# Triangular inversion from blocks of 16, finer bursts, and low parts on GpSimd in a recurrent stage

## The chip, the cores and the metric

One of a Trainium2 chip's cores runs the whole program. The metric is the device time of one execution in microseconds (us), the median of several runs. The engines are called PE (TensorE), DVE (VectorE), ACT (ScalarE), POOL (GpSimd) and SP (SyncE) in the profile.

## The reference, cut to what matters

Two transformer-like blocks work on 512 tokens of width 1024 in float32. The first block (two layers of attention and a gated feed-forward part) isn't touched by the change. The second holds an RWKV-7 time mix, a 31-tap causal convolution with a layer norm, a merge of both, and another feed-forward part:

```python
def wkv7(r, w, k, v, a, b):
    def step(S, inp):
        r_t, w_t, k_t, v_t, a_t, b_t = inp
        sa = jnp.einsum('bhvk,bhk->bhv', S, a_t)
        S = S * w_t[:, :, None, :] + sa[..., None] * b_t[:, :, None, :] + v_t[..., None] * k_t[:, :, None, :]
        y = jnp.einsum('bhvk,bhk->bhv', S, r_t)
        return S, y
    _, ys = lax.scan(step, S0, seq)
...
y_rwkv, v_first = rwkv7_time_mix(h, p_r, p_k, p_v, ...)
y_conv = conformer_conv(p_c, ...)
merged = jax.nn.sigmoid(z_rwkv) * y_rwkv + jax.nn.sigmoid(z_conv) * y_conv
x = x + rms_norm_2(merged @ w_out[i], post_mix_norm[i])
```

There are 16 heads of 64 columns. The kernel cuts the 512 steps of the scan into 8 chunks of 64 tokens. Within a chunk the steps become products with the inverse of a unit triangular 64x64 matrix, one for each head and chunk; between chunks the state S is carried on.

## The kernel before

**Products.** Float32 products are made of three passes in the float32r format: a weight tile `raw` is split into a high part `wh` (ScalarE copies it with rounding) and a low part `wl` (the rest, a subtraction). `wsplit` does this for weights, and the table `W["sub"]` says which engines take turns at the subtraction: VectorE alone outside of the recurrent stage, VectorE and GpSimd alternately in it. `dense` makes one unit of the stage: 24 products of 128x128 by 128x512 into one PSUM bank, 16 with the high part and 8 with the low part.

**The recurrent stage.** The function `tile_two_blocks` ends its second half with `drive`, which writes out the stage's order by hand. TensorE and VectorE keep the order in which the program issues their instructions. The table `units` lists 72 dense units in order: the convolution's inputs (c), the pairs of heads (i), the gates (g), the output maps of the time mix (w) and of the convolution (m). Between their products `drive` lets seven streams advance, as bursts of small instructions: `outs` (twice), which prepare one pair of heads each (`pair_out`); `solves`, which inverts the triangular matrices of a group of two pairs (`solve`, four groups); `chains`, which carries the state over 8 chunks (`chain`); `posts`, which normalizes a group's result; `mapped_rows`; and `ends`, which holds the convolution's layer norm. The w units need all four posts, apart from the first part of w0 and w1, which fill up the last chain; the m units need the layer norm.

**The planner's clock.** `Clock` holds a planned time for each engine, with a cost for each operation. A stream goes on when its last burst is done by that clock. `dense` yields after every second product, with True for a minor stop, at which streams that wait for a full burst (BURST or FREE) don't go on; full stops come where the count `n` of products is a multiple of 8. VectorE's spare time is given to the convolution's taps (`conv`, 8 x 30 multiply-adds on 128x512, tile `acc`): `taps.until(t)` issues taps as long as VectorE's planned end stays before `t`, which is TensorE's planned time minus 1 us. What GpSimd and ScalarE do follows from the order in which the streams issue it.

**The solve.** The diagonal 8x8 blocks of the matrices are gathered from a DRAM copy (`abd`) by four DMAs, inverted by forward substitution on VectorE (7 steps of a product and a sum, tile `x`), written back (`ttd`) and fetched as 32x32 blocks (`dd`, transposed `dt`). Then TensorE doubles the block size: `quad` makes 64 products of 32x32 (16 matrices on four 32-row strips), with the identity added in by a product of `ident` where `eye` is set. From 8 to 16 this takes the products dt,e and dd,de and de,dd; from 16 to 32 dt,RA and again dd,de and de,dd; from 32 to 64 the products RA and rr,dT. The tile `e` holds the entries of a 16x16 block that lie outside of its 8x8 blocks, scaled by a mask on ScalarE.

**The chain.** For each chunk: products of SV and X; ScalarE and VectorE copy half of the result each into SV; GpSimd scales the state (`ds`); products of SV and BKT; VectorE adds them to `ds` as the next SV; products with RA give the output.

**The layer norm's mean.** GpSimd adds each finished `acc` to `asum`. When all taps are done, a product with `oneD` makes the mean, VectorE subtracts it from 8 tiles, ScalarE squares them (`sq`), VectorE sums (`ssum`), and a product makes the variance.

The profile puts most instructions of the stage on a helper's lines: L192 is the recorder of TensorE's products, L152 that of the other engines, so groups are told apart by their tiles.

## Time and profile before

| | us |
|---|---|
| runs: median (lowest to highest) | 2426.93 (2425.42 to 2431.42) |
| profiled execution, own time | 2429.3 |
| its span | 2427.5 |
| TensorE, VectorE, ScalarE, GpSimd busy | 2313.3, 1198.5, 965.3, 339.0 |
| mean granted clock of TensorE | 0.969 of full speed |
| recurrent stage | about 1268 to 2005 |

The page begins with the busy time of each engine and its share of the span. "PEld" is TensorE's loading of weights, which runs beside its products. A row of the timeline has the start, the duration, the engine, the line, the operation with its tiles (output<-inputs), the shapes and the number of instructions merged in it; a bracket gives the engine's idle time ahead of it and what ended that. A row of the waits says who waited for whom. A product of float32 tiles that isn't split has two records in the profile.

### The profile page before, as it was taken

The page shows a single profiled execution, that of the slowest core. Times are in us where ns is not written, and L with a number is a line of the kernel's source. Part 1 is how long each engine was busy: PE and PEld are TensorE (multiplying, and loading weights), DVE is VectorE, ACT ScalarE, POOL GpSimd, SP SyncE. Part 2 cuts the span into 40 slices and gives each one's busy share as a digit, 9 for nine tenths or more (in the row PEclk, how much of TensorE's full clock was granted, in tenths as well). Part 3 has the DMA queues.
Part 4 walks back from the last instruction along what each step waited for, and adds up shares of the span by engine and source line. Part 5 has one row for each costly group of instructions (what it writes and reads, how often), then busy time and mean ns, then how long its engine had stood idle before and what let it go on. Part 6 is the DMA issues. An engine that isn't in the chain of part 4 may idle for free. (4 is left out here: it accounts for less than half of the span.)

```text
span 2427.5 us, 38347 instructions
## 1 busy us (share of the span) xinstructions
PE 2313.3 (95%) x15723; PEld 1862.5 (77%) x15723; DVE 1198.5 (49%) x1832; ACT 965.3 (40%) x1743; POOL 339.0 (14%) x457
## 2 busy tenths in 40 slices
PE   7899999999999999999999889999998699999998
PEld 6756788888798788888887677777776577888886
DVE  4366533234523653223355767778786655422232
ACT  4355423123434543222334645456633523322221
POOL 1000120000200000000012332354333221000000
PEclk9889999999999999999999899999999799999999
DMA  7330673224453144333232232234244254433331
GB/s 205 100 88 18 173 223 109 78 86 131 130 148 105 61 129 123 99 96 96 87 98 88 82 82 76 62 110 112 76 114 156 83 156 165 139 96 96 97 100 55
DMA packets 326543, 262.60 MB, mean 108 GB/s; under 512 B 47152, under 2 KB 294004, under 8 KB 325984
## 3 DMA queue, kind: packets, MB, share of 16 engines
q1 hardware_dynamic: 308552, 211.18, 29.9%
q10 hardware_dynamic: 9080, 22.37, 3.2%
q0 software_dynamic: 8736, 26.61, 3.1%
q8 instruction: 123, 2.02, 0.3%
q14 instruction: 52, 0.43, 0.1%
HBM read 225.81 MB, written 34.31 MB: 107 GB/s over the span
## 5 line engine op out<-in xcount | busy, mean ns | idle before, releaser
L186 PE MATMUL p<-hT_h,wh 128*128 128x512 f32 (+1 forms) x1376 | 511.8, 377 | 7.9 <-ACT qT L186 5.8
L186 DVE TENSOR_TENSOR wl<-raw,wh 128x1024 fp32r<-128x1024 f32 (+1 forms) x270 | 319.6, 1187 | 400.0 <-ACT wh L186 352.6
L186 PE MATMUL p<-hT_l,wh 128*128 128x512 f32 (+1 forms) x1376 | 511.4, 376 | 0.0
L186 ACT ACTIVATE wh<-raw 128x1024 fp32r<-128x1024 f32 (+1 forms) x270 | 275.8, 1025 | 547.6 <-PE p L186 370.6
L186 PE MATMUL p<-hT_h,wl 128*128 128x512 f32 (+1 forms) x1376 | 327.2, 375 | 0.0
L186 PEld LDWEIGHTS p<-hT_h,wh 128*128 128x128 f32 x1376 | 260.8, 190 | 56.3 <-ACT qT L186 6.2
L186 PEld LDWEIGHTS p<-hT_l,wh 128*128 128x128 f32 x1376 | 261.0, 190 | 46.9 <-issue 0.6
L186 PEld LDWEIGHTS p<-hT_h,wl 128*128 128x128 f32 x1376 | 247.5, 189 | 46.5 <-DVE wl L186 0.2
L186 POOL TENSOR_SCALAR rstd<-ss 128x1 f32<-128x1 f32 x52 | 18.6, 358 | 1467.0 <-ACT junk L186 1466.8
L152 DVE SCALAR_TENSOR_TENSOR acc<-c,dwc,acc 128x512 f32<-128x512 f32 x240 | 209.8, 877 | 6.7
L186 PE MATMUL p<-wh,fh 128*128 128x512 f32 x528 | 205.7, 390 | 0.7 <-DVE prm L186 0.7
L186 PE MATMUL p<-wl,fh 128*128 128x512 f32 x528 | 205.8, 390 | 0.0
L186 PE MATMUL p<-wh,fl 128*128 128x512 f32 x528 | 205.2, 389 | 0.0
L192 PE MATMUL p<-hT_h,wh 128*128 128x512 f32 x448 | 188.8, 421 | 2.9 <-ACT ls L152 2.1
L192 PE MATMUL p<-hT_l,wh 128*128 128x512 f32 x448 | 180.7, 403 | 0.6 <-issue 0.6
L186 DVE TENSOR_TENSOR fT<-sg,p 128x384 f32<-128x384 f32 (+1 forms) x88 | 46.8, 552 | 254.3 <-PE p L186 247.5
L192 PE MATMUL p<-hT_h,wl 128*128 128x512 f32 x448 | 120.6, 413 | 2.6 <-DVE wl L152 2.6
L152 ACT ACTIVATE wh<-raw 128x1024 fp32r<-128x1024 f32 (+1 forms) x78 | 77.4, 992 | 114.2 <-PE p L192 57.3
L186 DVE TENSOR_TENSOR fl<-fT,fh 128x512 fp32r<-128x512 f32 x66 | 45.1, 691 | 145.4 <-ACT fh L186 145.4
L186 PEld LDWEIGHTS p<-wh,fh 128*128 128x128 f32 x528 | 99.1, 188 | 21.5 <-ACT fh L186 0.9
L186 PEld LDWEIGHTS p<-wh,fl 128*128 128x128 f32 x528 | 99.1, 188 | 20.4
L186 PEld LDWEIGHTS p<-wl,fh 128*128 128x128 f32 x528 | 99.1, 188 | 20.3
(304 smaller groups left out, 3546.1 us busy)
## 6 DMA issues: line engine op xcount, KB each, us to landing
raw<-in_w_gu SPq DMA_DIRECT2D x88, 512.0 KB
raw<-in_w_in SPq DMA_DIRECT2D x56, 512.0 KB
raw<-in_w_down SPq DMA_DIRECT2D x44, 512.0 KB
raw<-in_ffn_w_gate SPq DMA_DIRECT2D x22, 512.0 KB
raw<-in_ffn_w_up SPq DMA_DIRECT2D x22, 512.0 KB
raw<-in_ffn_w_down SPq DMA_DIRECT2D x22, 512.0 KB
raw<-in_w_in_b SPq DMA_DIRECT2D x20, 512.0 KB
xs<-xt POOLq DMA_DIRECT2D x19, 512.0 KB, 4.2
```

Of the source, the lines that this page charges most:

```text
L152: return f(*a, **k)
L186: return f(*a, **k)
L192: return f(*a, **k)
```

## The change

It changes five things in the recurrent stage:

- The substitution on VectorE inverts 16x16 blocks: 15 steps of a product and a sum in place of 7, gathered and written back by two DMAs each in place of four, into tiles of 16x16 elements. The doubling from 8 to 16 goes, and with it the tile `e`, its scaled copies and the products dt,e and one dd,de and one de,dd of each solve.
- A full stop of `dense` comes after every fourth product.
- In the stage GpSimd alone makes the low parts.
- Taps are issued up to 1.5 us after TensorE's planned time.
- The planner's fixed cost of a tap (and of the other operations of that kind) goes from 0.21 to 0.26 us.

```diff
--- before.py
+++ after.py
@@ -125,7 +125,7 @@
             n, wide = math.prod(out.shape), len(out.shape) > 2 and out.shape[-1] < P
             return 0.65 if engine == "POOL" else 0.4 if not wide else 0.8 if n == 8192 else 0.65
         if engine == "DVE":
-            return (0.21 if op == "scalar_tensor_tensor" else 0.14) + n * (0.00215 if op.endswith("scan") else 0.00107)
+            return (0.26 if op == "scalar_tensor_tensor" else 0.14) + n * (0.00215 if op.endswith("scan") else 0.00107)
         if engine == "ACT":
             return 0.17 + n * 0.00086
         if op == "memset":
@@ -1008,7 +1008,7 @@
         i32 = blk[:, P + 1 : P + 33]
         centre = blk[:, P + 35 :]
         BANKS.update(ps=[0, 1, 2], po=[3, 4, 5], ca=[6], cb=[7])
-        W["sub"] = [nc.vector, nc.gpsimd]
+        W["sub"] = [nc.gpsimd]
         es2 = ExitStack()
         es2.enter_context(lows)
         el = es2.enter_context(tc.tile_pool(name="el", bufs=1))
@@ -1075,7 +1075,7 @@
                         nc.tensor.matmul(ps, lhsT=h[:, k, :], rhs=xl(k), start=False, stop=False)
                     n += 2 - part
                     if n % 2 == 0 and (n < 3 * len(ks) or len(ks) < KD):
-                        yield n % 8 != 0
+                        yield n % 4 != 0
             return ps
 
 
@@ -1319,9 +1319,9 @@
             def q32(i):
                 return slice(32 * i, 32 * i + 32)
 
-            def d8(t, r):
-
-                return bass.AP(t.tensor, t.offset + 264 * r, [[1024, 64], [32, 8], [1, 8]])
+            def d16(t, r):
+
+                return bass.AP(t.tensor, t.offset + 528 * r, [[1024, 64], [32, 16], [1, 16]])
 
             def quad(lhsT, rhs, eye=False):
 
@@ -1343,31 +1343,25 @@
             diag = [ABf[q32(i), :, q32(i % 2)] for i in range(4)]
 
             x = s2("x").rearrange("p q t -> p (q t)")
-            at, tt = (x[:, 128 * i : 128 * i + 128].rearrange("p (m a b) -> p m a b", m=2, a=8) for i in range(2))
-            pr = x[:, 256:]
-            nc.gpsimd.memset(tt, 0.0)
-            nc.gpsimd.memset(tt.rearrange("p m a b -> p m (a b)")[:, :, ::9], 1.0)
+            at, tt = (x[:, 256 * i : 256 * i + 256].rearrange("p (a b) -> p a b", a=16) for i in range(2))
+            pr = s2("pr").rearrange("p q t -> p (q t)")
+            nc.gpsimd.memset(x[:, 256:], 0.0)
+            nc.gpsimd.memset(x[:, 256::17], 1.0)
             yield from there(ab)
-            for r in range(4):
-                nc.sync.dma_start(at[64 * (r // 2) : 64 * (r // 2) + 64, r % 2], d8(ab, r))
-
-            e = s2("e")
-            nc.gpsimd.memset(e, 0.0)
+            for r in range(2):
+                nc.sync.dma_start(at[64 * r : 64 * r + 64], d16(ab, r))
+
             for i in range(4):
-                for m in range(2):
-                    cols = slice(16 * m + 8, 16 * m + 16)
-                    nc.scalar.activation(e[q32(i), :, cols], diag[i][:, :, cols], AF.Copy,
-                                         scale=blk[q32(i), P + 33 + m : P + 34 + m])
                 nc.gpsimd.memset(diag[i][:, :, 0:16], 0.0)
                 nc.scalar.activation(diag[i][:, :, 16:], diag[i][:, :, 16:], AF.Copy, scale=blk[q32(i), P : P + 1])
             yield from there(at)
-            for t in range(1, 8):
-                p4 = pr[:, : 2 * t * t].rearrange("p (m j s) -> p m j s", m=2, s=t)
-                nc.vector.tensor_tensor(p4, tt[:, :, :t, :t], at[:, :, None, :t, t].to_broadcast([P, 2, t, t]), ALU.mult)
-                nc.vector.tensor_reduce(tt[:, :, :t, t], p4, AX.X, ALU.add)
+            for t in range(1, 16):
+                p3 = pr[:, : t * t].rearrange("p (j s) -> p j s", s=t)
+                nc.vector.tensor_tensor(p3, tt[:, :t, :t], at[:, None, :t, t].to_broadcast([P, t, t]), ALU.mult)
+                nc.vector.tensor_reduce(tt[:, :t, t], p3, AX.X, ALU.add)
             yield from there(tt)
-            for r in range(4):
-                nc.sync.dma_start(d8(td, r), tt[64 * (r // 2) : 64 * (r // 2) + 64, r % 2])
+            for r in range(2):
+                nc.sync.dma_start(d16(td, r), tt[64 * r : 64 * r + 64])
             yield from there(td)
             dd, dt = s2("dd"), s2("dt")
             for i in range(4):
@@ -1376,15 +1370,6 @@
             nc.vector.transpose(dt, dd)
             yield BURST
 
-            de = s2("de")
-            nc.scalar.activation(de, quad(of(e), of(dt), True), AF.Copy)
-            yield BURST
-            dd_, dt = s2("dd"), s2("dt")
-            nc.scalar.activation(dt, quad(of(dd), of(de)), AF.Copy)
-            yield FREE
-            nc.scalar.activation(dd_, quad(of(de), of(dd)), AF.Copy)
-            dd = dd_
-            yield BURST
             de = s2("de")
             nc.scalar.activation(de, quad(lambda i: diag[i], of(dt), True), AF.Copy)
             yield BURST
@@ -1789,7 +1774,7 @@
             def stand():
                 t = clock.free("PE")
                 clock.t["PE"] = min([s[1] for s in streams if s[1] > t] + [t + 0.5])
-                taps.until(clock.t["PE"] - 1)
+                taps.until(clock.t["PE"] + 1.5)
                 burst()
 
             raws = [u[0]() for u in units[:2]]
@@ -1809,7 +1794,7 @@
                     if more and (at_ == SPLIT or (n == 3 and not units[i][4:])):
                         nxt, more = units[i + 1][1](raws.pop(0)), False
                     burst(at_ is True)
-                    taps.until(clock.free("PE") - 1)
+                    taps.until(clock.free("PE") + 1.5)
                 if more:
                     nxt = units[i + 1][1](raws.pop(0))
                 hl = nxt
```

The order of instructions moves throughout the stage. Three places follow, word for word as a listing of each engine's instructions has them; "..." stands for rows left out, and the number behind a tile tells buffers apart.

TensorE in the last solve, before; the rows with `SV`, `X` and `RA` are a chain's (`hT_h`, `wh`, `wl` are a dense unit's):

```order
L192 MATMUL p_15359<-blk,ident 128x512
L192 MATMUL p_15359<-dt,e 32x32 x64
...
L192 MATMUL p_15344<-RA_13394,SV_12896 64x64 x4
L192 MATMUL p_15453<-de,dd 32x32 x64
L192 MATMUL p_15329<-hT_h,wl 128x512 x8
L192 MATMUL p_15531<-SV_12896,X_12895 64x64 x4
L192 MATMUL p_15532<-X_12895,SV_12896 64x64 x4
L192 MATMUL p_15548<-dd,de 32x32 x64
...
L192 MATMUL p_15644<-blk,ident 128x512
L192 MATMUL p_15644<-dt,RA_14477 32x32 x64
```

The same place now:

```order
L192 MATMUL p_14867<-hT_l,wh 128x512
L192 MATMUL p_14874<-blk,ident 128x512
L192 MATMUL p_14874<-dt,RA_14046 32x32 x64
L192 MATMUL p_14941<-RA_12916,blk 128x512
...
L192 MATMUL p_14867<-hT_l,wh 128x512
L192 MATMUL p_14962<-de,dd 32x32 x64
L192 MATMUL p_14867<-hT_h,wh 128x512
...
L192 MATMUL p_15036<-dd,de 32x32 x64
```

The products dt,e and a first de,dd and dd,de are gone, the solve begins with dt,RA, and the pieces of a dense unit between its steps are four products long. Over the whole stage the 1728 large products stand in 126 pieces; they stood in 108.

VectorE at the end of the last chain, before (`acc` are taps, `SV` the chain's, `r` the last post's statistics, `asum` and `ssum` the layer norm's):

```order
L152 COPY SV_13826<-p_16621 64x2x64
L152 SCALAR_TENSOR_TENSOR acc<-c,dwc,acc 128x512
L152 TENSOR_TENSOR SV_13826<-p_16621,ds 64x2x64 x2
L152 SCALAR_TENSOR_TENSOR acc<-c,dwc,acc 128x512
L152 COPY SV_13826<-p_16649 64x2x64
L152 SCALAR_TENSOR_TENSOR acc<-c,dwc,acc 128x512 x3
L152 TENSOR_SCALAR r_16689<-p_16684 128x8
L152 TENSOR_SCALAR r_16696<-p_16691 128x8
L152 TENSOR_TENSOR RA_16389<-RA_16389,asum 128x512 x3
L152 TENSOR_TENSOR ssum<-ssum,sq 128x512
```

The same place now:

```order
L152 SCALAR_TENSOR_TENSOR acc<-c,dwc,acc 128x512 x2
L152 TENSOR_TENSOR SV_13419<-p_15777,ds 64x2x64 x2
L152 SCALAR_TENSOR_TENSOR acc<-c,dwc,acc 128x512 x2
L152 COPY SV_13419<-p_15823 64x2x64
L152 SCALAR_TENSOR_TENSOR acc<-c,dwc,acc 128x512 x7
L152 TENSOR_SCALAR r_15887<-p_15882 128x8
L152 TENSOR_SCALAR r_15894<-p_15889 128x8
L152 SCALAR_TENSOR_TENSOR acc<-c,dwc,acc 128x512 x2
L152 TENSOR_TENSOR RA_15581<-RA_15581,asum 128x512 x3
L152 TENSOR_TENSOR ssum<-ssum,sq 128x512
```

Nine taps stand behind the last copy of SV, where three stood, and two of them behind the statistics. On TensorE the last chain's first step stands after 1248 large products (before: 1272), its last one after 1360 (before: 1380).

GpSimd during the last chain, before (`ds` is the chain's scaled state, `wl` a low part, the DMA rows are stores):

```order
L152 TENSOR_TENSOR wl<-raw,wh 128x1024
L152 DMA zd_9677<-zsg 128x512
L152 TENSOR_TENSOR ds<-SV_13826,D_13828 64x128 x2
L152 DMA yd_9631<-RA_13394 128x512
L152 DMA zd_9678<-zsg 128x512
L152 TENSOR_TENSOR ds<-SV_13826,D_13828 64x128 x2
L152 DMA yd_9632<-RA_13394 128x512
L152 TENSOR_TENSOR ds<-SV_13826,D_13828 64x128 x2
L152 TENSOR_TENSOR wl<-raw,wh 128x1024
L152 DMA zd_9679<-zsg 128x512
L152 TENSOR_TENSOR ds<-SV_13826,D_13828 64x128
```

The same place now:

```order
L152 TENSOR_TENSOR ds<-SV_13419,D_13421 64x128 x2
L152 TENSOR_TENSOR wl<-raw,wh 128x1024
L152 DMA zd_9677<-zsg 128x512
L152 TENSOR_TENSOR ds<-SV_13419,D_13421 64x128 x2
L152 DMA ad_9663<-acc 128x512
L152 TENSOR_TENSOR asum<-asum,acc 128x512
L152 DMA zd_9678<-zsg 128x512
L152 TENSOR_TENSOR ds<-SV_13419,D_13421 64x128 x2
L152 TENSOR_TENSOR wl<-raw,wh 128x1024
L152 TENSOR_TENSOR ds<-SV_13419,D_13421 64x128 x2
L152 TENSOR_TENSOR wl<-raw,wh 128x1024
L152 DMA zd_9679<-zsg 128x512
```

There is a low part between most steps of the chain now. Of the stage's low parts of 128x1024, GpSimd makes 70 and all four of w_out's; it made 33 and two of w_out's.

## Rows read from the trace of the kernel before

**Rows 1.** Page, part 1, whole span: busy us (share) and instructions by engine
```profile
PE 2313.3 (95%) x15723; PEld 1862.5 (77%) x15723; DVE 1198.5 (49%) x1832; ACT 965.3 (40%) x1743; POOL 339.0 (14%) x457
```

**Rows 2.** Windows, recurrent stage: stretch; busy us by engine; clock, DMA share, GB/s
```profile
1268.00:2005.00 737.00, 674.34 (x7683) 527.84 (x7682) 516.65 (x755) 377.54 (x693) 249.81 (x275) 0.95 0.34 99
```

**Rows 3.** Waits of TensorE, 1268 to 2005: total us, times, longest
```profile
PE p L192 <- DVE ssum L152: 12.3, 1, 12.3
PE p L192 <- DVE RA L152: 10.6, 9, 3.1
PE p L192 <- DVE SV L152: 7.2, 6, 4.0
...
PE p L192 <- DVE wl L152: 5.4, 2, 2.8
```

**Rows 4.** Groups, TensorE, stage: busy us, mean ns | idle before
```profile
L192 PE MATMUL p<-de,dd 32*32 32x32 f32 x1024 | 11.4, 195 | 2.2 <-issue 2.1
L192 PE MATMUL p<-dd,de 32*32 32x32 f32 x1024 | 10.9, 193 | 1.5 <-issue 1.3
...
L192 PE MATMUL p<-blk,ident 128*128 128x512 f32 x16 | 8.7, 626 | 0.0
...
L192 PE MATMUL p<-dt,e 32*32 32x32 f32 x512 | 5.1, 193 | 0.0
```

**Rows 5.** Timeline, TensorE, undisturbed: start us, us, engine, line, operation
```profile
1409.02 1.98 PE L192 MATMUL p<-hT_h,wl 128*128 128x512 f32 x8
1410.84 0.39 PE L192 MATMUL p<-hT_h,wh 128*128 128x512 f32 x1
```

**Rows 6.** Timeline, TensorE, eight large products between bursts
```profile
1845.42 0.50 PE L192 MATMUL p<-hT_h,wh 128*128 128x512 f32 x1
...
1847.47 0.45 PE L192 MATMUL p<-SV,X 128*64 128x64 f32 x8
```

**Rows 7.** Timeline, VectorE, steps of the first solve
```profile
1393.53 0.16 DVE L152 TENSOR_TENSOR x<-x 128x2 f32<-128x2 f32 x1
1393.72 0.16 DVE L152 TENSOR_REDUCE x<-x 128x2 f32<-128x2 f32 x1
...
1400.05 0.33 DVE L152 TENSOR_TENSOR x<-x 128x98 f32<-128x98 f32 x1
1400.41 0.26 DVE L152 TENSOR_REDUCE x<-x 128x14 f32<-128x98 f32 x1
```

**Rows 8.** Groups by line, VectorE, stage
```profile
L152 DVE SCALAR_TENSOR_TENSOR acc<-c,dwc,acc 128x512 f32<-128x512 f32 x240 | 209.8, 877 | 6.7
L152 DVE TENSOR_TENSOR wl<-raw,wh 128x1024 fp32r<-128x1024 f32 x37 | 51.4, 1389 | 1.2 <-ACT wh L152 1.0
```

**Rows 9.** Groups by line, GpSimd, stage
```profile
L152 POOL TENSOR_TENSOR wl<-raw,wh 128x1024 fp32r<-128x1024 f32 x33 | 83.7, 2535 | 134.2 <-ACT wh L152 67.2 <-PE p L192 53.4 <-ACT RA L152 13.3
```

**Rows 10.** Timeline, VectorE, beside a low part on GpSimd
```profile
1555.90 4.32 DVE L152 SCALAR_TENSOR_TENSOR acc<-c,dwc,acc 128x512 f32<-128x512 f32 x3
...
1560.92 0.60 DVE L152 TENSOR_TENSOR SV<-p,ds 64x128 f32<-64x128 f32 x2
```

**Rows 11.** Timeline, GpSimd, the same stretch
```profile
1557.12 2.56 POOL L152 TENSOR_TENSOR wl<-raw,wh 128x1024 fp32r<-128x1024 f32 x1 [3.33 <-ACT RA L152]
```

**Rows 12.** Timeline, TensorE, same stretch (idle before it in brackets)
```profile
1561.67 0.45 PE L192 MATMUL p<-SV,X 128*64 128x64 f32 x8 [0.95 <-DVE SV L152]
```

**Rows 13.** Timeline, TensorE, end of the last chain and the layer norm
```profile
1879.80 0.45 PE L192 MATMUL p<-SV,BKT 128*64 128x64 f32 x8 [0.88 <-DVE SV L152]
...
1881.32 0.45 PE L192 MATMUL p<-SV,X 128*64 128x64 f32 x8 [0.69 <-DVE SV L152]
...
1901.81 1.87 PE L192 MATMUL p<-oneD,ssum 128*128 128x2 f32 x8 [12.29 <-DVE ssum L152]
```

**Rows 14.** Timeline, VectorE, the same end
```profile
1882.63 2.32 DVE L152 SCALAR_TENSOR_TENSOR acc<-c,dwc,acc 128x512 f32<-128x512 f32 x3
...
1894.20 0.69 DVE L152 TENSOR_TENSOR ssum<-ssum,sq 128x512 f32<-128x512 f32 x1 [2.63 <-ACT sq L152]
```

## The prediction

> **What bounds the kernel now.** I read the profile's first part, then the sums of the recurrent stage, then who TensorE waits for, then the rows of the instructions that the change touches. TensorE is busy for 95% of the span, every other engine for half of it or less [rows 1]. The change touches only the recurrent stage, which runs from about 1268 to 2005 us. There TensorE is busy for 674.3 of 737 us and VectorE for 516.7, at a mean granted clock of 0.95 [rows 2]. So most of the stage is bounded by the amount of work on TensorE, because large products fill what the recurrence leaves free; some 63 us are waits. The reader is to see in the waits that VectorE ends nearly all of the long ones, and that the largest, 12.3 us for ssum, lies in the layer norm at the end, where no product is left to fill with [rows 3].
>
> **The change part by part.** I count instructions in the order of before and of the change, take durations from the rows, and make the sum against the profiled execution's own time, 2429.3 us (span 2427.5 and 1.8 around it). The median of the runs, 2426.93, lies 2.4 below it.
>
> (a) *One doubling less.* Each of the four solves loses three of its six 64-matmul steps and one of two identity products. The profile counts twice as many records as instructions here. By their rows: all of dt,e (5.1 us), half of de,dd (11.4 busy and 2.2 waiting before them), half of dd,de (10.9 and 1.5), half of blk,ident (8.7) [rows 4]: 5.1 + 6.8 + 6.2 + 4.35 = 22.4 us. These lie between large products on the busy engine, with nothing beside them on TensorE, so I count all: **-22.4**. ScalarE loses the evacuations and the scaled copies, too; it is no bound here, so nothing is counted for them.
>
> (b) *Bursts after every fourth large product.* Counted in the order, the 1728 large products of the stage stood in 108 uninterrupted pieces and now stand in 126. Eight of them undisturbed take 1410.84 - 1409.02 = 1.82 us from start to start [rows 5], eight between two bursts 1847.47 - 1845.42 = 2.05 [rows 6]. An interruption costs 0.23 us: 18 x 0.23 = **+4.1**.
>
> (c) *Low parts on GpSimd.* 37 low parts of 128x1024 move within the stage (and two of w_out). TensorE waited twice for a low part that VectorE made, 5.4 us in all, the longer wait 2.8 [rows 3], and no wait of TensorE names one of GpSimd's 33, though these take 2535 ns against 1389 [rows 8, 9]. A low part is begun a whole unit ahead (24 products, 5.5 us undisturbed), which covers 2.5 us. I count the longer wait as gone: **-2.8**. GpSimd's queue is in order, and what stands behind a low part waits: the scaled state ds of the chain, the powers of the norms, and the stores that GpSimd issues itself. With 37 x 2.5 = 94 us more it is busy for some 345 of 737 us, under half.
>
> (d) *VectorE.* It loses 37 x 1389 ns = 51 us. It gains solve steps: 30 small operations for 14. From 2 and 98 elements, products take 0.16 and 0.33 us, sums 0.16 and 0.26 [rows 7], so per operation 0.16 us and about 1.8 or 1.0 ns an element. Over 1240 elements and 15 steps that is 4.6 + 3.7 us, with 0.03 between operations 9.2; over 280 elements and 7 steps 3.4. So +5.8 in each solve, +23 in all. And it is blocked: a tap takes 0.75 us alone, but three taps beside a GpSimd low part took 4.32 [rows 10, 11], 2.07 too many. Over the stage the taps' mean is 877 ns [rows 8]; their excess, 240 x 0.127 = 30 us, with 37 x 0.17 for VectorE's own low parts against 1.22 undisturbed, makes at most 1.1 us for each of 33 GpSimd low parts. 37 more give up to +41 us. VectorE ends at about 517 - 51 + 23 + 41 = 530 busy: the move frees nothing, and its idle 200 us must cover it. On TensorE's path the row to go by is the chain's SV at 1560.92, which stood behind the blocked taps; the product behind it started 0.95 late [rows 10, 12]. Upper end: every moved low part does that, 37 x 0.95 = 35 us. Lower end: half of the 17.8 us of waits on RA and SV go, since VectorE has fewer long operations, -9. The change also lets taps be queued until 1.5 us past TensorE's planned time in place of 1 before it, so 2.5 us or three more taps can stand ahead of a chain step. That moves me up from the middle of few cases seen; I take a quarter of the upper end, **+9**.
>
> The Trainium skill, "SBUF — State Buffer", section "SBUF: two separate sides", says that VectorE operations with two SBUF inputs and GpSimd operations contend for one shared port pair, held for the whole instruction, so that the loser blocks fully. The taps' row agrees (2.07 us lost beside a 2.56 us low part), and the rule speaks against this move; taken for all 37 at the rows' 2.5 us, it would block VectorE for 94 us in place of 41. By that the sum would come out near the second rival.
>
> (e) *The end of the recurrence.* The last chain's steps waited 0.88 and 0.69 us with no product left to fill [rows 13]; now 20 large products stand from its last step on. But nine taps stand behind the last copy of SV on VectorE, before only three, and the norm's mean needs them all: 6 x 0.75 = 4.5 us more, against 20 x 0.2275 = 4.6 us of products. The statistics of the last post now stand ahead of the mean on GpSimd and ScalarE, so the wait of 2.63 us for sq [rows 14] should go. The 12.3 us wait stays, about. Between -4 and +3; I take **-2**.
>
> The solve's small DMAs on SP's queue go from 32 to 16, each with four times the elements; SP issues weight loads beside them, and none of TensorE's waits names a transfer here, so 0 either way. The planner's edited cost of a tap (0.26 for 0.21) acts through the order alone.
>
> Sum: -22.4 + 4.1 - 2.8 + 9 - 2 = -14.1. 2429.3 - 14.1 = 2415.2; at the median's 2.4 lower, **2413 us**.
>
> **The rivals.**
>
> *VectorE is the bound of the stage's end.* Taps are the last thing before the layer norm, and VectorE's load does not fall. For it: the taps' end decides the mean in both orders, and the last chain moved ahead of the products by just 20 (from 1380 to 1360 of 1728). Against: 200 us of idle time. Then (a) ends as a wait for the taps and only (c), (e) and a few us remain: 2427 - 5 = 2422.
>
> *GpSimd blocks the chain (slower).* Low parts block taps, taps stand ahead of SV, and ds stands behind low parts in GpSimd's queue. Upper end of (d): -14.1 - 9 + 35 = +12, so 2439. It decides for more than (22.4 + 4.8 - 4.1)/37 = 0.62 us of TensorE wait per moved low part. For it: rows 10 to 12, and the deeper queue of taps. Against: one such row among dozens of low parts. The rule cited above is this rival's; the traces bear it out for the taps, not yet for TensorE.
>
> *More than forecast.* Finer bursts and less work shrink the early waits too; (d) at its lower end gives -14.1 - 18 = -32, so 2395.
>
> *The change does not do what it says*: the order shows the steps gone and the low parts moved, so I leave this at nothing.
>
> **How the numbers follow.** Forecast 0.55, VectorE bound 0.25, slower 0.12, more 0.08. The range leaves out most of the two extreme cases: 2399 to 2433. What a measurement can tell from no change is 0.3%, 7.3 us: faster is below 2419.6, slower above 2434.2. Forecast and its own spread give most of faster, with 0.08 of the better case and a fifth of the VectorE case: 0.64. Same takes the rest of the VectorE case and the forecast's upper tail: 0.24. Slower 0.12.
>
> **What would show it.** In the profile after: TensorE's 32x32 rows halved and 20 us fewer busy; no wait for a low part; VectorE's busy time in the stage within 20 us of before; taps' mean well above 877 ns; waits for SV and RA together no more than 27 us; the ssum wait still near 12. I am wrong if the waits for SV, RA and acc grow by over 25 us (second rival), if the mean's product waits for the taps for over 8 us (first), or if the low parts on GpSimd make TensorE wait.

## The result and the profile after

The change makes the kernel slower: 2445.44 us median of 4 runs (2439.05 to 2446.35) against 2426.69 (2425.42 to 2431.42) for the kernel before on the same chip, a ratio of 1.0065 (95% interval 1.0044 to 1.0085). Forecast was 2413, with 2433 as the upper end. It went the way of the rival "GpSimd blocks the chain", priced at 2439.

The profiled execution of the change took 2444.65 us (span 2442.9). Part 1 of its page answers to [rows 1]:

```profile
PE 2302.3 (94%) x14179; PEld 1851.9 (76%) x14179; DVE 1222.9 (50%) x1857; ACT 939.5 (38%) x1695; POOL 421.0 (17%) x492
```

TensorE has 1544 fewer instructions and is 11 us less busy, yet the span is 15 us longer, so TensorE must idle more. The stage, to its end some 15 us later (2020 for 2005), in the windows view; columns as in [rows 2]:

```profile
1268.00:2020.00 752.00, 664.21 (x6139) 518.75 (x6138) 540.13 (x779) 352.87 (x645) 331.76 (x311) 0.93 0.33 97
```

TensorE is busy for 10.1 us less and idle for 752 - 664.2 = 87.8 us, where it was 737 - 674.3 = 62.7: 25 us more idle. The granted clock is 0.93 for 0.95. If a stretch is either at 2.4 or at 1.2 GHz, that is some 105 us at the lower level in place of some 74, which takes part of the removed work back. Who TensorE waits for in that stretch, against [rows 3]:

```profile
PE p L192 <- DVE SV L152: 24.5, 15, 5.6
PE p L192 <- DVE RA L152: 15.8, 9, 4.1
PE p L192 <- DVE ssum L152: 10.4, 1, 10.4
PE p L192 <- ACT ls L152: 6.6, 1, 6.6
PE p L192 <- DVE BKT L152: 5.4, 1, 5.4
PE p L192 <- ACT SV L152: 4.5, 2, 2.4
PE p L192 <- POOL asum L152: 4.4, 1, 4.4
```

The waits for the chain's SV grew from 7.2 to 24.5 us, those for RA from 10.6 to 15.8; the wait for VectorE's low parts is gone. The groups of VectorE and GpSimd that answer to [rows 8, 9]:

```profile
L152 DVE SCALAR_TENSOR_TENSOR acc<-c,dwc,acc 128x512 f32<-128x512 f32 x240 | 236.7, 988 | 6.7
L152 DVE TENSOR_TENSOR pr<-x 128x1 f32<-128x1 f32 (+14 forms) x60 | 31.9, 532 | 1.9
...
L152 POOL TENSOR_TENSOR wl<-raw,wh 128x1024 fp32r<-128x1024 f32 x70 | 171.7, 2452 | 139.6 <-ACT wh L152 53.4 <-PE p L192 52.8 <-ACT RA L152 14.4
```

A tap takes 988 ns on average, before 877. How that reaches TensorE is seen in one place of the timeline, VectorE first (start, duration, idle before it in brackets):

```profile
1792.17 0.29 DVE L152 COPY SV<-p 64x128 f32<-64x128 f32 x1 [0.84 <-ACT SV L152]
1792.49 5.05 DVE L152 SCALAR_TENSOR_TENSOR acc<-c,dwc,acc 128x512 f32<-128x512 f32 x2
1797.57 0.61 DVE L152 TENSOR_TENSOR SV<-p,ds 64x128 f32<-64x128 f32 x2
```

GpSimd in the same stretch:

```profile
1791.67 2.40 POOL L152 TENSOR_TENSOR wl<-raw,wh 128x1024 fp32r<-128x1024 f32 x1
1794.01 0.58 POOL L152 DMA_DIRECT2D zd<-zsg  x1
1794.61 2.38 POOL L152 TENSOR_TENSOR wl<-raw,wh 128x1024 fp32r<-128x1024 f32 x1
```

And TensorE:

```profile
1795.25 0.40 PE L192 MATMUL p<-hT_l,wh 128*128 128x512 f32 x1
1798.33 0.70 PE L192 MATMUL p<-SV,X 128*64 128x64 f32 x8 [2.68 <-DVE SV L152]
...
1799.38 0.80 PE L192 MATMUL p<-hT_h,wh 128*128 128x512 f32 x1
1799.97 0.63 PE L192 MATMUL p<-hT_l,wh 128*128 128x512 f32 x1
1800.40 0.63 PE L192 MATMUL p<-hT_h,wh 128*128 128x512 f32 x1
```

Two taps that take 1.5 us undisturbed take 5.05 beside two low parts; the chain's SV stands behind them, and TensorE stands 2.68 us. Behind the gap its products run slower too, at first 0.59 and then 0.43 us apart instead of 0.23 [rows 5]. The windows around it show the clock:

```profile
1780.00:1798.00 18.00, 15.65 (x93) 12.12 (x92) 16.27 (x29) 4.87 (x8) 10.38 (x8) 1.00 0.45 127
1798.00:1804.00 6.00, 5.67 (x38) 4.47 (x38) 5.76 (x10) 1.49 (x3) 1.69 (x2) 0.72 0.61 167
```

The granted clock falls to 0.72 after the gap. Not every long wait is of this kind: the longest for SV (5.61 us, at 1857) stood behind a VectorE instruction that waited, by way of ScalarE's X, for a transfer from memory (yv), beside no low part.

### The profile page after: what moved, and what is told of

The parts are those of the page before. It is cut to its first block, busy times and chain, and to the rows that moved or that the text cites. A ratio compares the mean times of both kernels' runs of the same rounds, so it can differ in the third digit from the quotient of the medians.

```text
span 2442.9 us, 35242 instructions
## 1 busy us (share of the span) xinstructions
PE 2302.3 (94%) x14179; PEld 1851.9 (76%) x14179; DVE 1222.9 (50%) x1857; ACT 939.5 (38%) x1695; POOL 421.0 (17%) x492
## 5 line engine op out<-in xcount | busy, mean ns | idle before, releaser
L186 ACT ACTIVATE wh<-raw 128x1024 fp32r<-128x1024 f32 (+1 forms) x270 | 275.8, 1025 | 543.0 <-PE p L186 367.5
L152 DVE SCALAR_TENSOR_TENSOR acc<-c,dwc,acc 128x512 f32<-128x512 f32 x240 | 236.7, 988 | 6.7
L152 POOL TENSOR_TENSOR wl<-raw,wh 128x1024 fp32r<-128x1024 f32 x70 | 171.7, 2452 | 139.6 <-ACT wh L152 53.4
```

The costliest lines, as they stand in the source:

```text
L152: return f(*a, **k)
L186: return f(*a, **k)
```

## The experiments

Theories: A, GpSimd's low parts hold VectorE up and through it the chain; B, the taps that are queued 2.5 us deeper do; C, the finer bursts do; D, the longer substitution of the solve holds up what stands behind it on VectorE, and with it the taps' end and the mean. Ratios are against the kernel before, run on the same chip, and where two runs are compared, their ratios are. One profiled execution tells less: in the kernels here that don't differ ahead of the stage it began at 1267 to 1281 us, so where a time is read from a single trace it is the stage's own length, from its first instruction at line 192 to its last.

### One part undone, one part alone

*Low parts.* In no_pool the change's list goes back to both engines; in pool_alone the kernel before gets the change's list:

```diff
-        W["sub"] = [nc.vector, nc.gpsimd]
+        W["sub"] = [nc.gpsimd]
```

> The change with VectorE and GpSimd taking turns at the low parts again; the other parts stay. Theory A (GpSimd's low parts block VectorE's taps, and chain steps stand behind them): the 37 low parts that go back take most of the loss with them, about 25 us, so about 2420 us; the taps' mean falls from 988 ns toward 880 and the wait of TensorE for SV from VectorE at least halves. Theory B (the taps queued 2.5 us deeper are what delays the chain, whoever makes the low parts): within 6 us of the change, 2439 to 2451 us, and the waits for SV stay. Theory C (the full stops at every fourth product cost clock and mode changes): within 6 us of the change, and the half-clock periods of the stage stay as many.

> The kernel before with all low parts of the stage on GpSimd, nothing else. Theory D: the planner's VectorE is freer, taps end ahead of the last chain (240 of 240; before 218), the mean stands after 1272 large products in place of 1380: 10 to 20 us faster than before, about 2412 us, although VectorE is blocked more. Theory A: 37 more GpSimd low parts with up to 0.95 us of TensorE wait each: 10 us or more slower than before.

Measured: no_pool 2452.28, ratio 1.0091 (1.0060 to 1.0122); pool_alone 2445.81, 1.0067 (1.0050 to 1.0084). Low parts on GpSimd alone cost as much as the whole change, yet taking them back from it gains nothing. TensorE's waits in no_pool say why:

```profile
PE p L192 <- DVE wl L152: 24.0, 8, 6.6
...
PE p L192 <- DVE SV L152: 8.4, 8, 3.9
```

The waits for SV are back at 8.4 us (7.2 before), as A has it, and in their place TensorE waits for low parts on VectorE. The three longest of these waits, 18.1 of the 24.0 us, ended with a low part that VectorE began as soon as the substitution's last step was done. One of them, VectorE and then TensorE:

```profile
1647.35 0.39 DVE L152 TENSOR_REDUCE x<-pr 128x15 f32<-128x225 f32 x1
1647.66 1.22 DVE L152 TENSOR_TENSOR wl<-raw,wh 128x1024 fp32r<-128x1024 f32 x1
...
1648.93 2.07 PE L192 MATMUL p<-hT_h,wl 128*128 128x512 f32 x4 [6.60 <-DVE wl L152]
```

So A's number for no_pool (about 2420) was missed, through a wait that it had not looked for. In pool_alone the mean comes after 1272 products and the wait for ssum (12.3 us before) is gone; the loss of 16 us is what remains after that gain.

*The inversion.* no_inv puts blocks of 8 back into the change; inv_alone is the kernel before with blocks of 16 only (the middle of the diff above).

> The change with the inversion from blocks of 8 again; low parts on GpSimd, full stops at every fourth product and deeper taps stay. Theory D (the longer substitution is the cause: 23 us more on VectorE push the taps' end, and with it the layer norm's mean, behind the large products that would have covered it): by the order the taps end ahead of the last chain (240 of 240 at its first step; 201 in the change, 218 before), the mean's product stands after 1260 large products in place of 1380, so the wait for ssum goes wholly under products: 2426 - 20 = 2406 us, or 2420 if the waits for SV stay as in the change. Theory A (GpSimd's low parts block VectorE and the chain): still slower than before, 2435 us or more, with the taps' mean near 980 ns and over 20 us of waits for SV.

> The kernel before with the inversion from blocks of 16 alone. The working of the prediction's term (a): 22 us less work on TensorE and 23 us more on VectorE, so about 2427 - 20 = 2407 us. Rival: VectorE's longer substitution and the order that the planner makes of it give it back, within 5 us of the kernel before; then the 32x32 products were worth less than their busy time.

Measured: no_inv 2467.14, 1.0154 (1.0129 to 1.0180); inv_alone 2451.70, 1.0090 (1.0060 to 1.0119). On top of the rest the shorter inversion is worth 1.0154 - 1.0065, some 22 us, which is the size of term (a), though it is a net figure: in no_inv the mean also comes earlier, after 1260 products. D had no_inv at 2406 to 2420; as the cause of the change's loss it falls. Alone the shorter inversion loses 22. inv_alone waits for low parts on VectorE (5.4 us before):

```profile
PE p L192 <- DVE wl L152: 22.4, 6, 8.7
```

And the mean's product stands after 1536 of the 1728 large products instead of 1380, where it waits for the last taps; the wait for ssum behind it is not new (12.3 before). Both on its timeline:

```profile
1948.77 2.07 PE L192 MATMUL p<-asum,oneD 128*128 128x512 f32 x2 [9.61 <-POOL asum L152]
1961.26 1.84 PE L192 MATMUL p<-oneD,ssum 128*128 128x2 f32 x8 [10.42 <-DVE ssum L152]
```

*The taps.* no_taps puts the planner's limit and cost back; inv_taps is inv_alone with the change's limit and cost, and was run twice.

```diff
-                taps.until(clock.t["PE"] - 1)
+                taps.until(clock.t["PE"] + 1.5)
```

> The change with the taps' limit 1 us before TensorE's planned time and the planner's old cost of a tap; the other parts stay. Theory B (deeper queue of taps ahead of the chain's steps): at least 15 us faster than the change, below 2430 us, with the waits for SV at half or less, though the taps' mean stays near 980 ns. Theory A: blocked taps are fewer ahead of a chain step, but GpSimd blocks as before: 0 to 10 us faster. Theory C: within 6 us of the change.

> The inversion from blocks of 16 with the deeper taps (limit 1.5 us after TensorE's planned time, cost 0.26); low parts in turns, full stops at every eighth product. Theory D (the place of the mean among the large products sets the end): the mean stands after 1400 large products; with the inversion alone it stands after 1536, with its tail uncovered. So 12 to 20 us faster than the inversion alone (2451.7), about 2436 us. Theory B (deeper taps delay the chain): no faster than the inversion alone, with the waits for SV doubled.

> The same as inv_taps, again: inversion from blocks of 16 with the taps queued 2.5 us deeper and the low parts alternating between VectorE and GpSimd, bursts at every eighth product as before. Expected: the ratio to the kernel before stays at 0.997 to 1.000 (2421 to 2430 us). If it comes out above 1.002, the gain seen was the chip's scatter.

Measured: no_taps 2438.12, 1.0033 (1.0015 to 1.0051); inv_taps 2426.42, 0.9984 (0.9969 to 0.9999), again 2425.38, 0.9983 (0.9970 to 0.9996). In the change the deeper queue costs some 8 us by the ratios, but the two intervals overlap and the stage of the two profiled executions is about as long (738.0 and 737.2 us), so take it as 0 to 8. With it more blocked taps stand ahead of a chain step: TensorE's waits for SV are 24.5 us, and in no_taps half of that.

```profile
PE p L192 <- DVE SV L152: 12.5, 8, 5.9
```

Against that, in no_taps the mean comes only after 1488 products and waits 7.8 us for asum. With low parts on both engines the deeper queue gains some 26 us against inv_alone: the mean comes after 1400 products (1380 before). The deeper queue alone, in the kernel before, was not tried.

*The bursts.* no_burst goes back to every eighth product; burst_alone is the kernel before with every fourth.

```diff
-                        yield n % 8 != 0
+                        yield n % 4 != 0
```

> The change with full stops after every eighth product again; the other parts stay. Theory C (finer bursts: small instructions that come before VectorE is done with them, and more stretches at half clock): 15 us or more faster than the change, below 2430 us. Theory A (low parts on GpSimd) and theory B (deeper taps): within 6 us of the change.

> The kernel before with full stops at every fourth product, nothing else. The working of the prediction's term (b): more interruptions at 0.23 us each, about 4 us slower, and no more than 8. Rival (finer bursts shorten the chain and so the stage): 5 us or more faster. Theory C (finer bursts cost waits and clock): 10 us or more slower.

Measured: no_burst 2445.93, 1.0060 (1.0033 to 1.0086); burst_alone 2434.49, 1.0017 (0.9994 to 1.0041). Undone, nothing changes; alone, 4 us, which can't be told from none. C falls.

### What GpSimd's subtraction costs, and by which way

zero_low keeps the change's order on TensorE and VectorE and replaces the subtraction by writing zeros; it leaves the low parts of the stage's large weights out of the result:

```diff
+            if clock.on:
+                clock.op("POOL", "tensor_tensor", to(l), [fr(raw), to(h).bitcast(F32)],
+                         tc.nc.gpsimd.memset, (to(l).bitcast(F32), 0.0), {})
+                continue
```

> The change, with the order of TensorE and VectorE kept as it is; only GpSimd's subtraction that makes a low part in the recurrent stage is replaced by GpSimd writing zeros into the same tile, which reads nothing. Left out: the low parts of the large products' weights in that stage. Theory A (the subtraction holds VectorE's two-operand instructions up, and these hold up the copies of SV and RA that TensorE waits for): the mean tap goes from 988 ns to 800 or below, TensorE's waits for SV on VectorE in the stage from 24.5 us to under 10, and the time falls by 15 us or more against the change, to about 2430 or below. Rival B (the deeper queue of taps alone, whatever GpSimd does): waits for SV stay above 18 us and the time stays within 6 us of the change's 2445. Rival D (the longer substitution): the taps' end and the mean's product stand where they are in the order, so nothing moves either.

zero_busy writes the zeros two and a half times:

```diff
+                    for part in (z, z, z[:, : max(1, z.shape[1] // 2)]):
+                        tc.nc.gpsimd.memset(part, 0.0)
```

> As zero_low (low parts of the stage's large weights left out, set to zero), but GpSimd writes the zeros two and a half times over, so that each low part keeps it about 2.4 us, as long as the subtraction did, and it still reads nothing. Theory A1 (the subtraction's two tensor reads hold VectorE's two-operand instructions up): the mean tap stays under 830 ns and the time within 10 us of zero_low's 2384. Rival A2 (GpSimd's own order: the chain's products of the state with the decay, ds, stand behind 2.4 us of low part on GpSimd, whatever VectorE does): VectorE's waits for ds, 7.1 us in zero_low and 13.9 in the change, return to 12 or more, TensorE's waits for SV to 20 or more, and the time to 2425 or more.

Measured: zero_low 2383.96, 0.9812 (0.9787 to 0.9836); zero_busy 2389.36, 0.9827 (0.9803 to 0.9851). So the 70 subtractions cost the change 61 us by the runs, 0.88 each (0.80 by zero_busy). By the stage's length, 738.0 us in the change and 689.9 and 686.5 in these two, it is 48 and 52 us, 0.69 and 0.74 each. The price of one lies between 0.7 and 0.9 us. GpSimd is as long busy in zero_busy as in the change, and VectorE as free as in zero_low. GpSimd's and VectorE's groups in zero_busy:

```profile
L302 POOL MEMSET wl<- 128x1024 f32 (+1 forms) x210 | 170.5, 815 | 138.4 <-PE p L192 133.4
...
L152 DVE SCALAR_TENSOR_TENSOR acc<-c,dwc,acc 128x512 f32<-128x512 f32 x240 | 190.6, 795 | 6.8
L152 DVE TENSOR_TENSOR pr<-x 128x1 f32<-128x1 f32 (+14 forms) x60 | 20.7, 344 | 1.9
```

170.5 us of GpSimd against the change's 171.7, and a tap at 795 ns against 988. VectorE's waits for ds were 9.9 us here and 13.9 in the change, and TensorE's for SV stay at 10.7; the time did not return, and A2 falls:

```profile
PE p L192 <- DVE SV L152: 10.7, 6, 4.9
```

One way zero_busy leaves open: its low parts read nothing and so don't wait for ScalarE's high part first (53.4 us of idle time in the change's row above), and what stands behind them on GpSimd can start earlier. ScalarE's waits for ds fell, from 26.1 to 9.5 us. That this is not the main part is seen in no_burst, which makes all 70 low parts by subtraction and is as slow as the change, with waits for ds of only 14.0 us on ScalarE and 2.3 on VectorE.

TensorE's waits in zero_low, where in the change SV stood at 24.5 and RA at 15.8:

```profile
PE p L192 <- DVE SV L152: 10.8, 6, 4.9
...
PE p L192 <- DVE RA L152: 3.0, 4, 1.4
```

The rest of SV's waits (10.8, where under 10 was expected) is not the subtraction's. The stage's window in zero_low:

```profile
1268.00:1966.00 698.00, 645.07 (x6089) 503.45 (x6088) 448.42 (x778) 352.11 (x643) 222.91 (x311) 0.94 0.36 104
```

VectorE, with the same instructions, is busy for 540.1 - 448.4 = 92 us less, 1.31 us for each subtraction; what each costs TensorE (0.69 to 0.88) is half to two thirds of that. TensorE's idle time falls from 87.8 to 52.9 us.

### The substitution in pieces

inv_split is inv_alone, and inv_taps_split is inv_taps, with

```diff
             for t in range(1, 16):
...
+                if t in (7, 11, 13):
+                    yield
```

> The kernel before with the inversion from blocks of 16 alone, as in inv_alone, but the substitution hands VectorE back at three places (after steps 7, 11 and 13 of 15), so that no stretch of it is longer than about 5 us. Theory D, first half (TensorE waits for low parts on VectorE because they stand behind the substitution's 9 to 12 us in VectorE's queue): waits for wl fall from 22.4 us in inv_alone to under 12. Second half (the late end of the taps costs the uncovered layer norm): the mean's product stands at large product 1536 as in inv_alone, so the loss of some 38 us behind product 1440 stays, and the time is about 2440, 8 to 12 us under inv_alone's 2451.7. Rival: if the wl waits stay above 18 us, it is not the length of the substitution that they wait for.

> As inv_taps, with the substitution handing VectorE back at three places. D: waits for wl fall from 10.7 us to about 5, the waits for SV from 18 to about 14; against that the mean's product stands at large product 1480 instead of 1400, so some 80 products (about 19 us of cover at 0.23 us each) are missing behind it, of which inv_alone's 136 missing cost about 38. Expected: 2420 to 2440, most likely within 8 us of inv_taps either way; if the place of the mean's product decides, it is slower than inv_taps.

Measured: inv_split 2428.41, 1.0003 (0.9986 to 1.0020), 21 us better than inv_alone; inv_taps_split 2425.77, 0.9991 (0.9973 to 1.0009). TensorE in inv_split waits

```profile
PE p L192 <- DVE SV L152: 15.4, 9, 6.1
PE p L192 <- POOL asum L152: 12.2, 1, 12.2
PE p L192 <- DVE ssum L152: 10.4, 1, 10.4
PE p L192 <- DVE wl L152: 7.9, 4, 2.5
```

7.9 us for low parts, 22.4 in inv_alone: the first half of D holds. By the ratios the gain is larger than the 8 to 12 us forecast; the stage of the profiled execution is 11 us shorter (733.1 for 744.3).

The second half holds in direction, not in size. Counted along the large products, inv_split is 45 us ahead of the kernel before at the 1440th and 2 us ahead at the 1584th, but 12 of either come from a stage that began earlier, and between the two inv_split has its whole layer norm (its mean comes after 1536 products), which the kernel before has ahead of its 1440th (after 1380). So neither these 43 us nor the 38 that the expectation counted behind product 1440 are the price of a late mean. What is lost there are the waits for asum and ssum, 22.6 us for 12.3 before. With 8 more for SV and 2.5 more for low parts these make 21 us more than before: what the shorter inversion saves comes back as waits, about half of it at the taps' end. That VectorE bounds the end is the first rival's point, in a kernel other than the one it was made for.

### Low parts made earlier

pre_pool and pre_dve keep the whole computation; some 42 low parts are made in the feed-forward layers ahead of the stage, stored and loaded:

```diff
+            t = pp.tile([P, KD, P], F32R, tag="pret", name="pret")
+            nc.scalar.activation(t, raw, AF.Copy)
+            nc.vector.tensor_tensor(t, raw, t.bitcast(F32), ALU.subtract)
+            nc.gpsimd.dma_start(low, t.bitcast(F32))
...
+            nc.sync.dma_start(l.bitcast(F32), W["of"].pop(id(raw)))
```

> The inversion from blocks of 16, the taps queued 2.5 us deeper, bursts at every eighth product; some 42 of the stage's low parts are made two stages earlier, beside the two feed-forward layers' gate and up products (VectorE is about a third busy there), stored, and loaded in the stage; the other low parts of the stage on GpSimd, as in the change. Theory A, by 61.5 us for 70 low parts in zero_low against the change (0.88 us each): 42 fewer of them make it about 37 us faster than no_burst's 2446, near 2409; tap mean about 870. Rival: the added transfers (42 loads of 0.5 MB more and as many stores in the feed-forward layers, 42 loads in the stage) hold up the weights' loads and take it back; then TensorE waits on DMA or for wl in its queue, and the time stays above 2420.

> As pre_pool, but the low parts left in the stage are made by VectorE, none by GpSimd, and the substitution hands VectorE back at three places. Against inv_taps_split (2426) 33 low parts less on GpSimd at 0.88 us each, and some 9 fewer on VectorE: about 2395. If GpSimd's subtraction is what costs, it is faster than pre_pool; if VectorE's own time at the end of the taps decides, it is no faster than pre_pool and the mean's product waits for the taps.

Measured: pre_pool 2441.55, 1.0053 (1.0036 to 1.0070); pre_dve 2450.67, 1.0086 (1.0069 to 1.0104). From its first instruction at line 192 to its last the stage took 688 and 691 us, where before took 723 and the change 738: theory A's gain is there. But it began some 50 us late. ScalarE's waits in pre_pool from 500 to 1330 us name one cause:

```profile
ACT pret L186 <- DMA low<-pret: 99.1, 19, 6.4
```

The copy for the next early low part stood in ScalarE's queue until the last store had landed, and the gate's sigmoids behind it. pre_pool2 and pre_dve2 take two buffers and load one step earlier (`bufs=2` for `bufs=1`):

> As pre_pool, with two buffers each for the weights and low parts that are made early, and each load issued one step earlier. In pre_pool the recurrent stage took 688 us (before 723, the change 738), as theory A has it, but began 49 us late: ScalarE stood in the feed-forward layers before a copy into the only buffer, until the store of the last low part had landed (99 us after 500 us alone), and TensorE behind it for the gate's sigmoid product. If that is what took the gain back, the stage begins within 12 us of before's 1280 and the time is about 2400. Rival: the added 107 MB of transfers themselves slow the weights' loads; then it stays above 2420.

> The same two buffers and earlier loads in pre_dve (no low part on GpSimd in the stage, substitution handing VectorE back at three places). Its stage took 691 us against pre_pool's 688, so VectorE's own 28 low parts and GpSimd's 28 cost the same there. Expected: within 8 us of pre_pool2, about 2402; if the mean's product stands later in the order (1416 against 1380) and decides, 5 to 10 us slower than pre_pool2.

Measured: 2429.88, 0.9994 (0.9974 to 1.0013) and 2433.40, 1.0006 (0.9989 to 1.0023). Still 31 and 32 us late, so both missed their number; the gain of the stage was given back ahead of it. The single buffer was part of it: to 1290 us ScalarE's waits for the store fell from 178.4 in pre_pool to 37.4 in pre_pool2, while those for the feed-forward weights (raw<-in_w_gu) rose from 44.6 to 79.9 (60.4 in the kernel before). So the rival of added transfers has its part in it: pre_pool2's 2430 lies above 2420, its mark. By the page of its profile they are 68 MB, not 107. pre_pool3 lets the first six steps of each layer pass:

```diff
+                if f == 6 and order is not None:
+                    W["pre"] = early(es_pre)
```

> As pre_pool2, but the early low parts begin at the seventh of the 22 steps of each feed-forward layer, behind its first rush of weight loads, and so are 30 instead of 42; the other 40 are made by GpSimd in the stage. In pre_pool2 the stage began 31 us late, with TensorE's longest gaps at the start of the two layers (12.0 and 6.5 us, transfers there at 0.85 to 0.87 of the engines' time). Expected: the stage begins within 12 us of before's 1280, takes about 700 to 708 us (30 low parts at 0.88 us less than with all of them on GpSimd), and the time is 2410 to 2422, under the kernel before and the change. If the stage still begins over 20 us late, the early low parts cost TensorE through VectorE's and ScalarE's queues in those layers, not through the rush, and the time stays at 2430.

Measured: 2419.16 (2413.00 to 2422.93), 0.9958 (0.9941 to 0.9975). The stage begins 9 us late and takes 701 us, as expected. That is the best version with the whole computation: 10 us under the kernel before, 26 under the change. 40 low parts are still GpSimd's there, and a tap still takes 940 ns:

```profile
L152 POOL TENSOR_TENSOR wl<-raw,wh 128x1024 fp32r<-128x1024 f32 x40 | 98.7, 2466 | 76.2 <-PE p L192 35.9 <-ACT wh L152 30.9 <-ACT RA L152 7.9
L152 DVE SCALAR_TENSOR_TENSOR acc<-c,dwc,acc 128x512 f32<-128x512 f32 x240 | 225.3, 940 | 6.4
```

## Why the prediction was wrong, point by point

(a) One doubling less, -22.4: near the right size in the change. TensorE's rows after, against [rows 4]:

```profile
L192 PE MATMUL p<-dd,de 32*32 32x32 f32 x512 | 6.4, 204 | 4.9 <-ACT RA L152 2.1 <-issue 1.8 <-DVE RA L152 1.0
...
L192 PE MATMUL p<-de,dd 32*32 32x32 f32 x512 | 5.4, 193 | 1.2 <-issue 1.2
L192 PE MATMUL p<-blk,ident 128*128 128x512 f32 x8 | 5.3, 750 | 2.4 <-ACT SV L152 2.4
```

With dt,e gone, 36.1 us of busy time became 17.1. The idle time ahead of these rows, of which (a) counted half as gone, grew from 3.7 to 8.5, so the rows alone give 14 us. no_inv prices the inversion at a net 22 us. "I count all" holds only because the change also takes the low parts off VectorE: inv_alone shows it lost where they stay.

(b) Bursts, +4.1: burst_alone gave 4 us, no_burst none. Too small to have mattered.

(c) Low parts on GpSimd, -2.8: the wait for VectorE's low parts did go, and the one for GpSimd's is 1.3 us. What (c) missed is not in it: no_pool would wait 24 us for them, so the move also avoids a wait that the longer substitution would have made. The prediction put the substitution's 23 us on VectorE as load and did not look at what stands behind 9 us of it in one piece.

(d) VectorE, +9: **this is the step that failed**, "I take a quarter of the upper end". The mechanism was the right one and so was the row for it: the product that started 0.95 us late beside one low part [rows 10, 12]. The price measured per low part is 0.7 to 0.9 us, over 70 of them. For the 37 moved that is 26 to 33 us if all cost alike (the upper end had 35), and the deeper taps add up to 8 (no_taps), which the prediction had put into the same 9. pool_alone, which moves these 37 and nothing else, lost 16 us although its wait for ssum (12.3) went: 28 together, 0.77 each, an estimate. From the other side: the measured +15.8 (0.0065 of 2427) less the other terms' -23.1, as forecast, leaves 39 us for (d); 26 to 33 and up to 8 reach that. The argument against, "one such row among dozens", was read from single timeline rows; the sum, up to 1.1 us of VectorE's time for each low part, stood in the same text, and TensorE pays half to two thirds of what VectorE loses (0.69 to 0.88 of 1.31), not a small share.

VectorE's busy time was forecast at 530 and came out at 540, so its load was right; what it costs TensorE was not.

The Trainium skill, "SBUF — State Buffer", section "SBUF: two separate sides", says that a VectorE operation with two SBUF inputs contends for the shared port pair only against a GpSimd operation that reads SBUF. zero_busy agrees: the same 170 us of GpSimd without reads leave the tap at 795 ns, with reads it is 988.

(e) The end, -2: the wait for ssum is 10.4 (12.3 before), but one of 4.4 for the mean's sum stands ahead of it, since its taps now end at 1906.8, after the last products (1905.1). The prediction had the last post's statistics ahead of the mean as a help; on GpSimd they came in the way, as the last addition to asum stood behind them (r):

```profile
1904.60 3.70 POOL L152 TENSOR_TENSOR r<-r,neg_half 128x8 f32<-128x8 f32 x2 [11.62 <-DVE r L152]
1908.26 1.25 POOL L152 TENSOR_TENSOR asum<-asum,acc 128x512 f32<-128x512 f32 x1
```

The two waits together are 2.5 us longer; within (e)'s bounds, of the wrong sign.

The rivals. "GpSimd blocks the chain" decides above 0.62 us per moved low part; 0.7 to 0.9 lies above, and its 2439 is 6 us under what was measured. Its chance of 0.12 was too low for a mechanism of which the trace showed every link. "VectorE is the bound of the stage's end" did not decide here (4.4 us of wait, 8 was its mark); it did in inv_split. Of the signs, "waits for SV and RA together no more than 27 us" failed (40.3). Of the marks of error, "waits for SV, RA and acc grow by over 25 us" was just not reached (22.5), as the chain also waits through ScalarE (ls, SV and RA, 13.2 us for 4.2 before), which the mark left out.

What stays open: how much of the lower clock's some 31 us is the waits' doing, whether each of the 70 low parts costs alike, and what small part of their price goes by GpSimd's own order (ds) and not by VectorE.

## What to carry to other kernels

Before work is moved to an idle engine, look at what that engine's instruction does to those beside it, not at its busy share: here GpSimd, busy for 44% of the stage, cost TensorE some 50 to 60 us, most of it through VectorE. A blocked filler ahead of a chain step in an in-order queue is on the critical path; price it by the filler's excess over its undisturbed time, and count half to two thirds of that as lost. An edit that loses alone can gain beside another (the shorter inversion: 22 us lost alone, 22 gained with the low parts on GpSimd), so undo and add parts both ways before one is blamed.

## What the runs showed of the hardware

Of VectorE's groups, those that grew by over 1.5 us beside GpSimd's subtraction have two or more inputs, all in SBUF. Between zero_low and the change, the 240 taps went from 191.6 to 236.7 us, the 60 products pr from 20.8 to 31.9, the 8 sums RA<-RA,bv from 5.9 to 11.0. The 56 SV<-p,ds, with one operand in PSUM, took 16.1 in both, and 32 X<-p,tri 22.0. The same tile written by GpSimd without reading (0.96 us each in zero_low, 2.44 in zero_busy) slowed none of them: of VectorE's rows here, it is the reads of GpSimd that hold them up.
